# Hybrid decoder step on one core: order of the Winograd products, of the weights' sums and loads, of a tile ring, and of the opening

## Chip, cores, metric

The kernel runs on one core of one Trainium2 chip, as one launch. The metric is the device time in microseconds, as the median of several executions. TensorE is called PE here, its weight loads PEld, VectorE DVE, ScalarE ACT, GpSimd POOL and SyncE SP, as in the profile.

## The reference

One inference step of a decoder layer in fp32: 16 meta rows and a prompt of 512 rows, and 8 sample rows, model width 2048.

```
hp = layer_norm([meta; x_prompt]);  hs = layer_norm(x_sample)
z  = h @ w_in + b_in        -> q (16 x 64) | k (4 x 64) | v (4 x 64) | pool input u (1024)
a  = sliding-window attention with sinks;  p = multi-scale causal pooling of u
h1 = layer_norm(ALPHA * h + [a, p] @ w_o)
ff = (silu(h1 @ w_gate) * (h1 @ w_up)) @ w_down      # 2048 -> 5632 -> 2048
y  = layer_norm(ALPHA * h1 + ff)
```

It returns y of the prompt and of the samples, the last 128 rotated keys and values, and the last 15 pooling inputs.

## The kernel before

**Precision.** Each fp32 product is made of three passes in a faster fp32 format: an operand is split into a high and a low part, and `products` (L200 to L206) issues weight-high x data-high (L203), weight-high x data-low (L204), weight-low x data-high (L206). `split` (L183) makes the parts of 512 weight columns: the high part is a ScalarE copy (L187), the low part a VectorE subtraction (L188). They go into a ring of five slots each (`WB`), taken in the order of the code.

**Stages.** Opening (normalise x, transpose it, k and v projections, 0 to some 60 us); q and u projections with attention and pooling; output projection and first normalisation (to some 530 us); the gate and up projections (to 1457 us); the down projection (to 1875 us); last normalisation.

**Opening.** The loop over h (two halves of the columns) and g (four groups of rows of w_in), n = 4h + g + 1, places per round: `x_split` of an odd pair of row blocks (VectorE L372, ScalarE L375 and L378, VectorE L379), `x_norm` (ScalarE L341), `kv_mm`, the transposes `x_turn`, splits of three weight blocks, `x_split` of an even pair, `kv_mm`, the split of the fourth block. Each `step` keeps its instructions on PE, VectorE and ScalarE behind those of the step before. `later` holds the statistics of the row blocks 2 and 3 (VectorE L310, two at each `next`), which `normalisers(1)` and `x_norm(1, 0)` need.

**Gate and up.** 44 column blocks are taken as 22 pairs; each pair has a gate set g and an up set u. A `Set` multiplies a 2 x 2 block of weights (four tiles of 128 x 1024 floats, `q(r, c)`, loaded by L180 into `raw`, a ring of six slots) with 2 x 2 blocks of h1 in the Winograd form of Strassen: seven products P1 to P7, each of 8 x 3 = 24 matmuls of 128 x 260. The data operands are ready (`bop`: b11, b21, b22, t1 to t4, which P1, P2, P3, P5, P6, P7, P4 use). The weights need four sums on VectorE (`weight_sum`, L196), made in place of a loaded tile: S3 = A11 - A21 for P7, one from it for P6, one for P5, one for P3. Banks of PSUM: `al` holds P1, then P6, P5, P3 in turn; `ga` holds P7, then P4; `de` holds P2. VectorE or ScalarE reads a bank after a product, and a product that adds to it or starts it anew must come behind that read: L1024 reads P7 (`c22 = ga + p1`), L1030 P6, L1038 P2, L1043 P5, L1047 P4, L1052 P3.

Three kinds of sets: g0 and u0 are *kept* (P1 and P2 were made ahead and stand in PSUM); the up sets u1 and those of the next nine pairs are *filled* (P1 was made ahead and stands in SBUF, so six products are left); all others make seven. The order in the code of `run` before: kept P7 P6 P5 P4 P3, filled P2 P7 P6 P4 P5 P3, others P1 P7 P6 P2 P5 P4 P3.

**What sets the order on an engine.** A list scheduler of the framework orders each engine's instructions when the kernel is built, by readiness in its own timing and by priority; loads, splits and sums are raised by 400 instructions (`WPRIO`). `weight_sum` also stays behind the last low part that was split before it in the code. So an engine's order can differ from that of the code: PE in fact takes P2 of a gate set before its P6 where the input of P6 is late. The queue of loads on SP is one line, in the scheduler's order.

**Rows.** `row_tile` takes rows of 520 floats from a ring of 16 slots for x, later for z1 and, with 14 slots (`bufs`), for the gate and up stage: eight rows a pair (two of `go`, p of g, two of `uo`, p of u, `t12` and `t34`), six in the pairs of PLAIN, the last two. Slots are handed out in turn from `rows[2]`.

**Down.** `load_w(c, j)` (L1197, L1203) loads the weights of one column pair and, for c = 0, the two h1 tiles of accumulator j, which take the place of rows (accumulator j stands where slots 2j and 2j + 1 stood). `load_ops` (L1186) loads the operands into the 56 slots of `bop`. These all stand in one order on SP: `load_w(0, 0)`, ten operands, `load_w(0, 1)`, 25 operands, `load_w(0, 2)`, `load_w(0, 3)`. `column_pair` makes seven products of 15 matmuls; two column pairs start interleaved.

Of the kernel before, what the change touches and what calls it, by code (L numbers as in the profile page):

```python
# [31 lines left out]
NPAIR = F_TILES // 2  # L32
# [35 lines left out]
def hybrid_step(ctx, tc, xin, w_in, w_o, w_g, w_u, w_d, w_pool, par_d, cst_d, ident_d, ln2gb, kct_d, vc_d, hist_d,  # L68
                ck_d, cv_d, sp_d, yp, ys, nkp, nvp, npp, nks, nvs, nps):
    nc = tc.nc  # L70
# [184 lines left out]
    with ExitStack() as sa:  # L255
# [185 lines left out]
        for h in range(2):  # L441
            for g in range(4):
                n = h * 4 + g + 1
                with step(*three):
                    x_split(h, 2 * g + 1)
                    if n < 8 and n != 4:
                        x_norm(n // 4, n % 4)
                with step(*three):
                    kv_mm(h, 2 * g)
                if n < 8:  # L450
                    with step(*three):
                        x_turn(n // 4, n % 4)
                        if n < 7:
                            load_kvw((n + 1) % 4)
                        kvw.pop(n % 4, None)
                        kv_weights(n % 4, range(3))
                if h == 0 and g < 2:
                    with step(*three):
                        next(later.pop(0))
                if n < 8:  # L460
                    with step(*three):
                        x_split(n // 4, 2 * (n % 4))
                if n == 2:
                    with step(*three):
                        for x in later:
                            next(x)
                if n == 3:
                    with step(*three):
                        norm[1] = normalisers(1)
                        x_norm(1, 0)  # L470
                with step(*three):
                    kv_mm(h, 2 * g + 1)
                    if n < 8:
                        kv_weights(n % 4, [3])
            with step(*three):
                for i in range(4):
                    if i % 2:
                        nc.vector.tensor_scalar(zkv[i][:, XH[h]], out[i], par[:, PBIAS + i:PBIAS + i + 1], None,
                                                op0=ALU.add)
                    else:  # L480
                        nc.scalar.activation(zkv[i][:, XH[h]], out[i], AF.Identity, bias=par[:, PBIAS + i:PBIAS + i + 1])
                if h == 0:
                    out = kv_banks(1)
# [467 lines left out]
    class Set:  # L951


        def __init__(self, w, i, name):
            self.w, self.i, self.name = w, i, name
            self.raw, self.bk, self.p1 = {}, {}, None

        def q(self, r, c):
            if (r, c) not in self.raw:
# [4 lines left out]
        def s(self, t, a, b, op):  # L964
            weight_sum(op, self.q(*t), self.q(*a), self.q(*b))
            return self.q(*t)

        def prod(self, n, bk, first=True):


            b = {1: "b11", 2: "b21", 3: "b22", 4: "t4", 5: "t1", 6: "t2", 7: "t3"}[n]
            src = {1: lambda: self.q(0, 0), 2: lambda: self.q(0, 1), 4: lambda: self.q(1, 1),
                   7: lambda: self.s((1, 0), (0, 0), (1, 0), nc.vector.tensor_sub),
                   6: lambda: self.s((1, 0), (1, 1), (1, 0), nc.vector.tensor_sub),
                   5: lambda: self.s((0, 0), (1, 0), (0, 0), nc.vector.tensor_add),
                   3: lambda: self.s((0, 1), (0, 1), (1, 0), nc.vector.tensor_sub)}[n]()
            for g in range(2):
                wh, wl = split(src[:, g * 512:(g + 1) * 512], f"{self.name}_{n}{g}")
                for kk in range(4):
                    k = 4 * g + kk  # L980
                    sl = slice(kk * P, (kk + 1) * P)
                    hi, lo = bop[b][k // 2]
                    products([bk], wh[:, sl], wl[:, sl], [hi[:, k % 2, :]], [lo[:, k % 2, :]], k == 0 and first, k == 7, True)
# [17 lines left out]
        def run(self, c11, c12, c21, c22, side=(), out=None):  # L1001
# [12 lines left out]
                al = bank(f"p1_{self.name}")  # L1014
            ga = bank(f"p7_{self.name}")
            next(side, None)
            if filled and de is None:

                de = bank(f"p2_{self.name}")
                self.prod(2, de)  # L1020
            self.prod(7, ga)
            next(side, None)
            if filled:
                nc.vector.tensor_add(c22, ga, self.p1)  # L1024
            else:
# [2 lines left out]
            next(side, None)  # L1028
            if filled:
                nc.vector.tensor_add(c21, al, self.p1)  # L1030
                self.prod(4, ga, False)
            else:
                nc.scalar.copy(c21, al)
                if de is None:
                    de = bank(f"p2_{self.name}")
                    self.prod(2, de)
            next(side, None)
            nc.vector.tensor_add(c11, de, self.p1)  # L1038
            if out:
# [1 line left out]
            self.prod(5, al, False)  # L1041
            next(side, None)
            nc.vector.tensor_add(c22, c22, al)  # L1043
            if not filled:
                self.prod(4, ga, False)
            next(side, None)
            nc.vector.tensor_add(c21, c21, ga)  # L1047
# [68 lines left out]
        bop[n] = [(slot(f"{n}h{i}"), slot(f"{n}l{i}")) for i in range(4)]  # L1116
    turn = [i for i in range(NPAIR) if i not in PLAIN] + [*PLAIN]
    sets = [Set(w, i, f"{n}{i}") for i in turn for n, w in (("g", w_g), ("u", w_u))]
    g1 = ln1(1, zs1)
    fills = [s.ahead(n) for n in (1, 2) for s in sets[:NKEEP]]  # L1120
    for j, s in enumerate(sets[NKEEP + 1::2][:NFILL]):
# [20 lines left out]
    nxt = raws[2] % NRAW  # L1142
    raws[0] = raws[0][nxt:] + raws[0][:nxt] + [(fr, end[0])]
    raws[2] = 0
    rows[0] = [x for x in order if x[1] not in end]
    rows[2] = 0
    bufs.update(raw=NRAW + 1, row=14)
    side = ()
    for j, i in enumerate(turn):
# [362 lines left out]
```

## Time and profile before

| | us |
|---|---|
| three runs, median (lowest to highest) | 1950.8 (1949.04 to 1953.36) |
| the profiled execution | 1951.08 |
| its span, first to last instruction | 1949.3 |
| PE busy | 1897.8 |
| DVE busy | 1545.2 |
| ACT busy | 936.7 |
| mean granted clock of TensorE, share of full | 0.993 |

Times in the trace are counted from the start of the span. Matmuls are pipelined and their ends are modelled: a matmul of 128 x 260 is shown as 0.28 us long, while one starts every 0.12 us, so an idle time printed in front of a matmul is some 0.16 us shorter than what was lost from start to start. In a timeline a line is start, length, engine, line of the code, operation, out<-in, count, and in brackets the idle time of the engine before it with what ended it. In a list of stretches the five busy times are of PE, PEld, DVE, ACT and POOL.

### The profile page before, as it was taken

The numbers are of one execution on the slowest core, as the hardware profiler recorded it, in microseconds if no ns is written. First come the engines' busy times: TensorE is split into PE (matmuls) and PEld (weight loads), VectorE is DVE, ScalarE is ACT, GpSimd is POOL, SyncE is SP. The second block draws the span as 40 slices with busy tenths as digits, with TensorE's granted clock in tenths as the row PEclk, the third lists the DMA queues.
The fourth block names the chain that finished last, engine by engine and source line by source line (L and its number), as shares of the span: only waits on it lengthen the run. The fifth ranks groups of instructions, "written<-read, shape, count | busy, mean of one in ns | idle before, by whom it ended". The sixth has DMA issues, their size and how long they took to land.

```text
span 1949.3 us, 39269 instructions
## 1 busy us (share of the span) xinstructions
PE 1897.8 (97%) x15533; PEld 1867.3 (96%) x15533; DVE 1545.2 (79%) x2734; ACT 936.7 (48%) x1808; POOL 2.7 (0%) x9
## 2 busy tenths in 40 slices
PE   8999999999999999999999999999998999999996
PEld 8999999999989999999999999999998999999996
DVE  6765657768678888888888888888867888888878
ACT  6644445545555444444455555555544433443441
POOL 0000000000000000000000000000000000000000
PEclk9999999999999999999999999999999999999998
DMA  8722222766754545454545445453539564655232
GB/s 268 240 96 73 65 80 72 223 200 198 226 173 163 163 142 165 134 180 135 170 137 181 135 148 162 145 172 126 184 129 399 200 219 167 224 174 202 93 98 88
DMA packets 145240, 319.27 MB, mean 164 GB/s; under 512 B 14288, under 2 KB 66232, under 8 KB 144952
## 3 DMA queue, kind: packets, MB, share of 16 engines
q1 hardware_dynamic: 144480, 315.71, 48.9%
q8 instruction: 122, 2.00, 0.4%
q10 hardware_dynamic: 576, 1.05, 0.2%
q14 instruction: 62, 0.51, 0.1%
HBM read 265.22 MB, written 54.03 MB: 164 GB/s over the span
## 4 chain that ended last, share of the span: by engine, by line
PE 88%; DVE 5%; DMA 2%; ACT 2%; issue 1%; ACTq 0%; SPq 0%; DVEq 0%
PE p_g L203 7%; PE p_g L204 7%; PE p_g L206 7%; PE tri L206 6%; PE tri L203 6%; PE p_u L203 6%; PE tri L204 6%; PE p_u L204 6%; PE p_u L206 6%; PE o L203 3%; PE o L206 3%; PE o L204 3%; PE p_u L990 2%; DVE rr L188 2%; PE mm_u L203 2%; PE mm_u L206 2%
## 5 line engine op out<-in xcount | busy, mean ns | idle before, releaser
L187 ACT CAST rr<-fr 128x512 fp32r<-128x512 f32 (+1 forms) x1056 | 654.4, 643 | 807.5 <-DVE fr L196 269.2
L188 DVE TENSOR_TENSOR rr<-fr,rr 128x512 fp32r<-128x512 f32 (+1 forms) x1056 | 734.4, 716 | 252.2 <-ACT rr L187 238.8
L196 DVE TENSOR_TENSOR fr<-fr 128x1024 f32<-128x1024 f32 (+1 forms) x304 | 319.4, 1051 | 27.7 <-DMA fr<-in_w_u_dram 21.6
L203 PE MATMUL p_g<-rr 128*128 128x260 f32 x830 | 235.3, 285 | 7.9 <-ACT rr L187 6.4
L206 PE MATMUL p_g<-rr 128*128 128x260 f32 x830 | 230.6, 282 | 0.0
L203 PE MATMUL p_u<-rr 128*128 128x260 f32 x770 | 218.2, 284 | 6.5 <-DVE fr L1024 6.3
L204 PE MATMUL p_g<-rr 128*128 128x260 f32 x788 | 221.7, 282 | 0.0
L206 PE MATMUL p_u<-rr 128*128 128x260 f32 x770 | 215.2, 282 | 0.0
L204 PE MATMUL p_u<-rr 128*128 128x260 f32 x748 | 210.8, 283 | 0.0
L203 PE MATMUL tri<-rr 128*128 128x260 f32 x696 | 198.1, 285 | 4.9 <-ACT rr L187 3.9
L206 PE MATMUL tri<-rr 128*128 128x260 f32 x696 | 197.6, 284 | 1.9 <-DVE rr L188 1.9
L204 PE MATMUL tri<-rr 128*128 128x260 f32 x696 | 197.4, 284 | 0.0
L203 PEld LDWEIGHTS p_g<-rr 128*128 128x128 f32 x830 | 156.2, 188 | 10.2 <-ACT rr L187 8.5
L206 PEld LDWEIGHTS p_g<-rr 128*128 128x128 f32 x830 | 155.1, 189 | 0.0
L203 PEld LDWEIGHTS p_u<-rr 128*128 128x128 f32 x770 | 144.9, 188 | 8.1 <-issue 8.1
L204 PEld LDWEIGHTS p_g<-rr 128*128 128x128 f32 x788 | 148.1, 188 | 0.0
L203 PE MATMUL o<-rr 128*128 128x260 f32 x512 | 145.0, 284 | 0.3 <-ACT rr L187 0.3
L206 PEld LDWEIGHTS p_u<-rr 128*128 128x128 f32 x770 | 144.7, 189 | 0.0
L204 PE MATMUL o<-rr 128*128 128x260 f32 x512 | 144.0, 282 | 0.0
L206 PE MATMUL o<-rr 128*128 128x260 f32 x512 | 143.6, 282 | 0.2 <-DVE rr L188 0.2
L204 PEld LDWEIGHTS p_u<-rr 128*128 128x128 f32 x748 | 140.7, 188 | 0.0
L203 PEld LDWEIGHTS tri<-rr 128*128 128x128 f32 x696 | 131.8, 189 | 5.4 <-ACT rr L187 5.4
(320 smaller groups left out, 4564.4 us busy)
## 6 DMA issues: line engine op xcount, KB each, us to landing
fr<-in_w_u_dram SPq DMA_DIRECT2D x100, 512.0 KB
fr<-in_w_g_dram SPq DMA_DIRECT2D x90, 512.0 KB
fr<-in_w_d_dram SPq DMA_DIRECT2D x64, 640.0 KB
t_d<-fr SPq DMA_DIRECT2D x140, 260.0 KB
fr<-in_w_o_dram SPq DMA_DIRECT2D x64, 512.0 KB
fr<-in_w_in_dram SPq DMA_DIRECT2D x48, 512.0 KB
rr<-t_d SPq DMA_DIRECT2D x87, 260.0 KB
mid_b<-t_d SPq DMA_DIRECT2D x53, 260.0 KB
```

The lines of the kernel that those rows point to most:

```text
L187: nc.scalar.copy(wh, s)
L188: last_lo[0] = (lo or nc.vector).tensor_sub(wl, s, wh.bitcast(F32)).ins
L196: i = op(*args).ins
L203: nc.tensor.matmul(o, wh, hi[j], start=first, stop=False, skip_group_check=onto)
L204: nc.tensor.matmul(o, wh, lo[j], start=False, stop=False, skip_group_check=onto)
L206: nc.tensor.matmul(o, wl, hi[j], start=False, stop=last, skip_group_check=onto)
L990: nc.tensor.matmul(bk, self.q(0, n - 1)[:, k * P:(k + 1) * P], z1[0][4 * (n - 1) + k // 2][:, k % 2, :], start=(k == 0), stop=(k == 7))
```

## The change

In the gate and up stage a set may make S3 early (`early`): an unfilled set while P1's weights are split, between the two halves; a filled or kept set while P3 of the set before it is split. Filled sets begin with P7 and then P2; kept sets take P4 ahead of P5. With S3 early, a filled set loads its tiles in the order A21, A11, A12, A22 instead of A12, A21, A11, A22. The ring of rows is put in the order of addresses and starts at slot 10 (-172 modulo 14), so that the last row handed out is the last slot. In the opening the statistics of row blocks 2 and 3 and the second normalisation move behind the second `kv_mm` and the last split of their round, one, two and one `next` in the first three rounds.

```diff
--- before.py
+++ after.py
@@ -454,24 +454,20 @@
                             load_kvw((n + 1) % 4)
                         kvw.pop(n % 4, None)
                         kv_weights(n % 4, range(3))
-                if h == 0 and g < 2:
-                    with step(*three):
-                        next(later.pop(0))
                 if n < 8:
                     with step(*three):
                         x_split(n // 4, 2 * (n % 4))
-                if n == 2:
-                    with step(*three):
-                        for x in later:
-                            next(x)
-                if n == 3:
-                    with step(*three):
-                        norm[1] = normalisers(1)
-                        x_norm(1, 0)
                 with step(*three):
                     kv_mm(h, 2 * g + 1)
                     if n < 8:
                         kv_weights(n % 4, [3])
+                if n < 4:
+                    with step(*three):
+                        for _ in range((1, 2, 1)[g]):
+                            next(later.pop(0))
+                        if n == 3:
+                            norm[1] = normalisers(1)
+                            x_norm(1, 0)
             with step(*three):
                 for i in range(4):
                     if i % 2:
@@ -953,7 +949,7 @@
 
         def __init__(self, w, i, name):
             self.w, self.i, self.name = w, i, name
-            self.raw, self.bk, self.p1 = {}, {}, None
+            self.raw, self.bk, self.p1, self.s3, self.next = {}, {}, None, False, None
 
         def q(self, r, c):
             if (r, c) not in self.raw:
@@ -965,17 +961,27 @@
             weight_sum(op, self.q(*t), self.q(*a), self.q(*b))
             return self.q(*t)
 
+        def early(self):
+
+            self.s((1, 0), (0, 0), (1, 0), nc.vector.tensor_sub)
+            self.s3 = True
+
         def prod(self, n, bk, first=True):
 
 
             b = {1: "b11", 2: "b21", 3: "b22", 4: "t4", 5: "t1", 6: "t2", 7: "t3"}[n]
             src = {1: lambda: self.q(0, 0), 2: lambda: self.q(0, 1), 4: lambda: self.q(1, 1),
-                   7: lambda: self.s((1, 0), (0, 0), (1, 0), nc.vector.tensor_sub),
+                   7: lambda: self.q(1, 0) if self.s3 else self.s((1, 0), (0, 0), (1, 0), nc.vector.tensor_sub),
                    6: lambda: self.s((1, 0), (1, 1), (1, 0), nc.vector.tensor_sub),
                    5: lambda: self.s((0, 0), (1, 0), (0, 0), nc.vector.tensor_add),
                    3: lambda: self.s((0, 1), (0, 1), (1, 0), nc.vector.tensor_sub)}[n]()
             for g in range(2):
                 wh, wl = split(src[:, g * 512:(g + 1) * 512], f"{self.name}_{n}{g}")
+                if g == 0 and n == 1:
+                    self.early()
+                if g == 0 and n == 3 and self.next and (self.next.p1 is not None or self.next.bk):
+
+                    self.next.early()
                 for kk in range(4):
                     k = 4 * g + kk
                     sl = slice(kk * P, (kk + 1) * P)
@@ -1014,12 +1020,12 @@
                 al = bank(f"p1_{self.name}")
             ga = bank(f"p7_{self.name}")
             next(side, None)
-            if filled and de is None:
-
+            self.prod(7, ga)
+            next(side, None)
+            kept = de is not None
+            if filled and not kept:
                 de = bank(f"p2_{self.name}")
                 self.prod(2, de)
-            self.prod(7, ga)
-            next(side, None)
             if filled:
                 nc.vector.tensor_add(c22, ga, self.p1)
             else:
@@ -1028,12 +1034,13 @@
             next(side, None)
             if filled:
                 nc.vector.tensor_add(c21, al, self.p1)
+            else:
+                nc.scalar.copy(c21, al)
+            if filled or kept:
                 self.prod(4, ga, False)
             else:
-                nc.scalar.copy(c21, al)
-                if de is None:
-                    de = bank(f"p2_{self.name}")
-                    self.prod(2, de)
+                de = bank(f"p2_{self.name}")
+                self.prod(2, de)
             next(side, None)
             nc.vector.tensor_add(c11, de, self.p1)
             if out:
@@ -1041,7 +1048,7 @@
             self.prod(5, al, False)
             next(side, None)
             nc.vector.tensor_add(c22, c22, al)
-            if not filled:
+            if not (filled or kept):
                 self.prod(4, ga, False)
             next(side, None)
             nc.vector.tensor_add(c21, c21, ga)
@@ -1116,6 +1123,8 @@
         bop[n] = [(slot(f"{n}h{i}"), slot(f"{n}l{i}")) for i in range(4)]
     turn = [i for i in range(NPAIR) if i not in PLAIN] + [*PLAIN]
     sets = [Set(w, i, f"{n}{i}") for i in turn for n, w in (("g", w_g), ("u", w_u))]
+    for a, b in zip(sets, sets[1:]):
+        a.next = b
     g1 = ln1(1, zs1)
     fills = [s.ahead(n) for n in (1, 2) for s in sets[:NKEEP]]
     for j, s in enumerate(sets[NKEEP + 1::2][:NFILL]):
@@ -1142,8 +1151,9 @@
     nxt = raws[2] % NRAW
     raws[0] = raws[0][nxt:] + raws[0][:nxt] + [(fr, end[0])]
     raws[2] = 0
-    rows[0] = [x for x in order if x[1] not in end]
-    rows[2] = 0
+
+    rows[0] = sorted((x for x in order if x[1] not in end), key=lambda x: x[1])
+    rows[2] = -(6 * NPAIR + 2 * (NPAIR - len(PLAIN))) % 14
     bufs.update(raw=NRAW + 1, row=14)
     side = ()
     for j, i in enumerate(turn):
```

## Rows read from the trace of the kernel before

**Rows 1.** The page: busy shares (part 1), VectorE's low parts (part 5)

```profile
PE 1897.8 (97%) x15533; PEld 1867.3 (96%) x15533; DVE 1545.2 (79%) x2734; ACT 936.7 (48%) x1808; POOL 2.7 (0%) x9
...
L188 DVE TENSOR_TENSOR rr<-fr,rr 128x512 fp32r<-128x512 f32 (+1 forms) x1056 | 734.4, 716 | 252.2 <-ACT rr L187 238.8
```

**Rows 2.** Stretches: us, busy us (instructions) of each engine, granted clock, DMA share, GB/s

```profile
1025.12:1428.12 403.00, 403.00 (x3360) 403.00 (x3361) 341.41 (x525) 213.40 (x408) 0.00 (x0) 1.00 0.47 155
...
590.70:1025.12 434.42, 420.00 (x3458) 416.12 (x3456) 375.24 (x594) 212.72 (x403) 0.00 (x0) 1.00 0.48 154
...
1457.07:1514.86 57.79, 49.69 (x376) 48.26 (x377) 40.47 (x57) 25.50 (x39) 0.00 (x0) 0.94 0.99 383
...
1514.86:1778.07 263.21, 263.21 (x2198) 263.21 (x2197) 223.37 (x314) 107.48 (x151) 0.00 (x0) 1.00 0.59 205
...
749.27:1025.12 275.85, 265.74 (x2184) 263.04 (x2184) 238.16 (x379) 132.86 (x253) 0.00 (x0) 1.00 0.48 155
...
618.60:641.58 22.98, 22.98 (x194) 22.98 (x193) 20.48 (x34) 12.70 (x24) 0.00 (x0) 1.00 0.59 196
```

**Rows 3.** Waits of PE, whole span: us in total, times, longest us

```profile
PE p_g L203 <- ACT rr L187: 6.4, 10, 0.6
...
PE p_u L203 <- DVE fr L1024: 6.3, 7, 1.1
```

**Rows 4.** Timeline of one filled up set: PE, VectorE (start, us; idle before)

```profile
755.43 0.28 PE L203 MATMUL p_g<-rr 128*128 128x260 f32 x1
...
757.63 1.23 DVE L196 TENSOR_TENSOR fr<-fr 128x1024 f32<-128x1024 f32 x1 [2.46 <-DMA fr<-in_w_u_dram]
...
765.98 1.22 DVE L196 TENSOR_TENSOR fr<-fr 128x1024 f32<-128x1024 f32 x1
...
767.12 0.42 DVE L1024 TENSOR_TENSOR fr<-p_u,fr 128x260 f32<-128x260 f32 x1
...
767.69 0.36 PE L203 MATMUL p_u<-rr 128*128 128x260 f32 x1 [0.80 <-DVE fr L1024]
```

**Rows 5.** Timeline of the SP queue around one filled pair

```profile
730.21 0.33 SPq L180 DMA_DIRECT2D fr<-in_w_u_dram  x1
...
751.33 0.51 SPq L180 DMA_DIRECT2D fr<-in_w_u_dram  x1
...
770.76 2.38 SPq L180 DMA_DIRECT2D fr<-in_w_g_dram  x2
```

**Rows 6.** Timeline of one gate set: ScalarE and PE at P4

```profile
748.60 0.62 ACT L187 CAST rr<-fr 128x512 fp32r<-128x512 f32 x1 [0.81 <-PE p_g L204]
...
749.27 0.39 PE L203 MATMUL p_g<-rr 128*128 128x260 f32 x1 [0.64 <-ACT rr L187]
```

**Rows 7.** Timeline of g0: VectorE and PE before P3

```profile
602.42 1.22 DVE L196 TENSOR_TENSOR fr<-fr 128x1024 f32<-128x1024 f32 x1
...
603.55 0.42 DVE L1043 TENSOR_TENSOR fr<-fr,p_g 128x260 f32<-128x260 f32 x1
...
604.12 0.36 PE L203 MATMUL p_g<-rr 128*128 128x260 f32 x1 [1.49 <-DVE fr L1043]
```

**Rows 8.** Timeline of the SP queue, last set and after

```profile
1429.75 20.84 SPq L1203 DMA_DIRECT2D fr<-h_d  x2
...
1450.69 2.28 SPq L1186 DMA_DIRECT2D rr<-t_d  x5
...
1456.53 1.03 SPq L1197 DMA_DIRECT2D fr<-in_w_d_dram  x2
```

**Rows 9.** Timeline of PE, start of the down projection

```profile
1463.60 0.59 PE L203 MATMUL tri<-rr 128*128 128x260 f32 x1 [3.18 <-ACT rr L187]
...
1497.03 0.39 PE L203 MATMUL tri<-mid_b,rr 128*128 128x260 f32 x1 [1.80 <-DVE fr L1230]
```

**Rows 10.** Timeline of VectorE and PE in the opening

```profile
25.83 1.28 DVE L310 BATCH_NORM_STATS2 mid_a<-fr 128x6 f32<-128x512 f32 x2
...
28.36 0.53 PE L203 MATMUL kv<-rr 128*128 128x276 f32 x2 [0.96 <-ACT rr L378]
```

## Prediction

> **What bounds the kernel now.** The page comes first: PE is busy for 97% of the span [rows 1], so a change can win only what PE loses in places. The question is where PE loses time, and the stretches answer it [rows 2]. With two unfilled sets a pair, from 1025.12 to 1428.12 us, PE runs 3360 matmuls in 403.00 us, 0.1199 us each, with no idle time: that is the pace when nothing is missing, and 24 matmuls (one product) are 2.88 us. The earlier stretch, 590.70 to 1025.12, where the up sets of ten pairs are filled, holds 3458 matmuls in 434.42 us. At 0.1199 they are 414.8, so **19.7 us are lost**. The third stretch is the start of the down projection: 376 matmuls in 57.79 us, where the steady down projection has 2198 in 263.21 (0.1198 each, 45.0 for 376). There **12.8 us are lost**, at a granted clock of 0.94.
>
> Who ends the waits [rows 3]: first matmuls of gate products wait ten times for a ScalarE high part (L187), of up products seven times for VectorE's L1024. The reader is to see that these are two causes with one period: seven pairs take 275.85 us, 39.4 each, against 312 x 0.1199 = 37.4 [rows 2], so 2.0 us a pair.
>
> **The change part by part.** The number of products, sums, splits and loads is unchanged, so all of it is order.
>
> *Up sets begin with P7.* In a filled up set P4 restarts the bank of P7, which L1024 must have read. The order on PE is P2, P7, P6, P4, so L1024 has one product (2.88 us). At 767.69 PE waits for it: VectorE was idle up to 757.63 for a load, then had splits and sums in a row, the last one at 765.98, ahead of L1024 at 767.12 [rows 4]. After the change the order is P7, P2, P6, P4: L1024 has two products, 5.76 us, and needed 2.88 plus 0.80. So this wait goes. Its sum: the 19.7, less the gate waits and the one of g0 below, is 8.5 us. What is late next is L1030, which must read P6's bank before P5 adds to it, with one product (P4) between, as before. I take 7.5 us, bounds 3 (L1030 inherits part of it) and 8.5.
>
> *S3 one product ahead.* Before, S3 of an up set waits 2.46 us for a load [rows 4]. The raw ring has six slots and a set takes four: the first two loads go into slots that have been free for a whole set, the third and fourth into those of the set just ending. The queue shows it: for this set (0,1) was issued at 730.21, while (0,0), its third, left at 751.33 [rows 5]. The new order of loads is (1,0), (0,0), (0,1), (1,1), so S3's two inputs come 20 us early and the late one belongs to P2, one product later. S3 itself (1.22 us of VectorE) only moves: in front of the second low part of P3 (or of P1, in unfilled sets), where splits run ahead of PE.
>
> *The gate waits.* At 749.27 PE needs the first high part of P4, and ScalarE makes it only at 748.60, when a product has let go of its slot [rows 6]. That slot, five splits back, was P6's second half. P6 ran last because its input (1,1) came late: it goes into the slot of the up set's first load, (0,1), which is free only after the last split of that set, and the two loads of this kind leave at 770.76 and after 772.8 [rows 5]. After the change the first load is (1,0), which the sum of P3 lets go, some 2 us earlier. The one gate set in the stretch whose predecessor already loads in the new order is g1, behind the kept u0: 194 matmuls in 22.98 us, no idle time [rows 2]. Start to start the wait is 0.92, and the next two matmuls are late by 0.15 together: 0.95 us, ten times, 9.5. I take 7.5; bounds 0 (order on PE and slots unchanged) and 9.5.
>
> *Kept sets.* In g0 the sum for u0's P7 (602.42) stands ahead of L1043 (603.55), on which P3 waits until 604.12: 1.49 us idle, 1.65 over the pace [rows 7]. S3 made a product ahead stands before the end of P5 and no longer there; L1043 still lies open between P5 and P3, 0.42 and the way there. I take 1.0, bounds 0 and 1.65.
>
> *Row ring.* The SP queue is one line. At 1429.75 it issues half of the first accumulator's h1, then stands 20 us for a row that the last up set still uses; the ten operand loads start at 1450.69, the weights of the second column pair at 1456.53 [rows 8]. PE waits for these weights until 1463.60 [rows 9] and the clock falls. Turned, the last pair has rows 8 to 13, and rows 0 to 7, which the accumulators 0 to 3 take, are free a pair (40 us) earlier. The next thing the queue waits for is the operands' own slots: b11 after P1 of the last set, about 1439.8 (1457.07 [rows 2] less 6 products of 2.88 us), t3 after P7, 1442.7, and so on. So the loads start 11 us earlier, over a DMA system that is nearly idle, and keep ahead: five operands of 260 KB in 3.6 us of two interleaved products are 370 GB/s, and the stretch moved 383 [rows 2]. What stays: the first split of the new pool waits for the last matmul of the old one (about 1.2 us), and the bursts of two pairs starting together on VectorE (the wait on L1230 at 1497.03, 1.80 us [rows 9], is of that kind). I take 9.0 of the 12.8 us; bounds 5 and 11.
>
> The Trainium skill ("DMA: Bandwidth & Descriptors", Specifications) puts what a core gets from HBM at about 358 GB/s. By that the 22.1 MB of this stretch (57.79 us at 383 GB/s) would take 61.8 us, 4 us more, which the head start would still cover; the trace shows more than the page allows, and the row decides.
>
> *Opening.* The statistics of the later rows move behind x_split and the last split of a step. At 25.83 they hold up x_split by 1.28 us, and PE waits 0.96 at 28.36 [rows 10]; that goes. But the same work then stands, undiminished, before the next x_split, and the normalisers and x_norm now come behind the last split instead of ahead of it. VectorE's chain through this stretch keeps its length but for that, so most is given back by 52 us. I take 0.5; bounds -0.5 and 2.
>
> *Sum.* 7.5 + 7.5 + 1.0 + 9.0 + 0.5 = 25.5 us. The profiled execution took 1951.1 us (span 1949.3), 0.3 over the median of 1950.8, so 1925.3 on the median.
>
> **Rivals.** *The gate waits stay*, since slots and not loads set them: P4's first part still finds P6's slot taken. For it: a pattern alike to the hundredth ten times over. Against: g1. 1925.3 + 7.5 = 1932.8.
>
> *L1030 takes L1024's place*: it has the slack L1024 had, and VectorE does 238.16 us in seven pairs, 34.0 of what would then be 37.4, 91% against 85% (341.41 of 403.00) where nothing is lost [rows 2]. Against: its backlog came from the 2.46 us wait. 1932.8 as well.
>
> *The start of the down projection is bound by VectorE*, not by loads, and gives back 4: 1930.
>
> *The schedule in the pair stays as it is*: the order on each engine is made by a list scheduler with weight work raised in priority, and may come out with the old waits. Then only the row ring and opening pay: 1950.8 - 9.5 = 1941.3.
>
> *Slower: S3 blocks VectorE.* It is queued ahead of P3's second low part. If it waited for a load as it does now (until 757.63 [rows 4]), that part would be ready at 757.63 + 1.22 + 0.72 (a split's low part [rows 1]) = 759.6, where PE, in P3 from 755.43 [rows 4], needs it after 14 matmuls, at 757.1: 2.5 us in each of ten pairs, 25 us. With the gate waits kept, 1950.8 - 9.0 - 0.5 - 7.5 + 25 = 1958.8. It decides from the point where the second load lands after 757.1 - 0.72 - 1.22 = 755.2. The issue times of [rows 5] speak against it by some 20 us. The Trainium skill ("PSUM — Partial Sum Buffer", Engine vs sequencer instructions) calls VectorE's queue a strict FIFO, the rule by which this would happen; the trace agrees, since L1024 sat behind a sum it does not need.
>
> **How the numbers follow.** Forecast 1925 at 0.46; gates stay 0.17; L1030 0.13; VectorE at the down start 0.10; schedule unchanged 0.08; slower 0.06. All low bounds together save 3 + 0 + 0 - 0.5 + 5 = 7.5 (1943), all high ones 8.5 + 9.5 + 1.65 + 11 + 2 = 32.7 (1918). The range 1917 to 1941 leaves out the slower case and part of the unchanged one. Measurement tells 0.2%, 3.9 us, from no change; every case but the slower one is past it, with a little kept for partial mixtures: faster 0.91, same 0.03, slower 0.06.
>
> **What would show it.** Right: a filled pair of 37.5 to 38 us instead of 39.4, no wait on L1024, no p_g wait of 0.64 before P4; operand loads from about 1440 and no PE idle over 1.5 us at 1457 to 1500, clock 1.00. Wrong: up sets waiting at P7 on an L187 or L196; a wait on L1030 of like size; VectorE idle for a load between P3's two low parts; operand loads still issued after 1450.

## The result, and the profile after

The changed kernel takes **1932.4 us** (median of 4 runs, 1931.94 to 1932.89) against 1950.6 for the kernel before in the same runs: a ratio of 0.9905, 95% interval 0.9888 to 0.9922. That is 18.2 us less. The forecast was 1925, 25.5 us less. The profiled execution took 1932.89 us, its span 1931.1.

Divided at the starts of the same matmuls (g0's first; the 3459th from there, which lies in the gate set behind the last filled pair, just behind that set's wait before P4; the first and the 377th of the down projection, and so on), the profiled executions stand like this, in us:

| stretch | before | after | difference |
|---|---|---|---|
| first transpose to the end of the opening | 80.15 | 80.39 | +0.24 |
| from there to g0 | 494.48 | 494.50 | +0.02 |
| filled pairs, with the kept pair ahead of them (3458 matmuls) | 434.77 | 426.37 | -8.40 |
| unfilled pairs | 432.27 | 432.28 | +0.01 |
| start of the down projection (376 matmuls) | 57.23 | 47.21 | -10.02 |
| the next 2198 matmuls | 263.56 | 263.56 | 0 |
| last stretch | 155.90 | 156.16 | +0.26 |

So two stretches paid, and they are the two that the forecast named. First the page of the changed kernel (part 1, PE's line) and the stretches (us, busy us and instructions of each engine, then granted clock, DMA share and GB/s):

```profile
PE 1894.4 (98%) x15533; PEld 1865.8 (97%) x15533; DVE 1539.9 (80%) x2734; ACT 944.1 (49%) x1808; POOL 2.7 (0%) x9
```

```profile
15.89:96.28 80.39, 76.94 (x585) 74.33 (x585) 58.36 (x111) 52.86 (x99) 0.00 (x0) 0.94 0.77 249
...
590.78:1017.15 426.37, 418.83 (x3460) 416.00 (x3459) 370.36 (x593) 214.41 (x402) 0.00 (x0) 1.00 0.50 157
1017.15:1449.43 432.28, 431.54 (x3601) 431.33 (x3599) 362.81 (x558) 232.68 (x437) 0.00 (x0) 1.00 0.49 163
1449.43:1496.64 47.21, 45.90 (x376) 45.31 (x377) 37.09 (x53) 23.26 (x35) 0.00 (x0) 1.00 0.96 355
```

The down projection starts at full clock now (1.00, 0.94 in [rows 2]). In the filled pairs 3458 matmuls at 0.1199 us would be 414.6, so 11.8 us are still lost there. The waits of PE in that stretch (us in total, times, longest) say to what:

```profile
PE p_g L203 <- ACT rr L187: 7.1, 11, 0.6
PE p_g L203 <- ACT fr L1038: 0.3, 1, 0.3
PE p_u L203 <- ACT rr L187: 0.2, 1, 0.2
```

The waits on L1024 and L1043 of [rows 3, 7] are gone. (The change moves lines: what was L1024, the addition of P7's bank and the kept P1, is L1030 after.) The gate waits of [rows 3] are not: they were ten and are **eleven**, at the same 0.64 us. The new one is g1's, the very set on whose lack of a wait the forecast leaned.

L1030 (old L1024) in one filled up set, VectorE's timeline: its bank is read at 684.05, and P4 restarts the bank at 688.55 without a wait.

```profile
684.05 0.42 DVE L1030 TENSOR_TENSOR fr<-p_u,fr 128x260 f32<-128x260 f32 x1
...
688.55 0.28 PE L203 MATMUL p_u<-rr 128*128 128x260 f32 x1
```

The SP queue at the start of the down projection, which [rows 8] show of before (start us, us for issuing, line): the ten operands leave at 1429.31, 20.1 us ahead of the first matmul (1449.43); before, 7.1 us ahead (1450.69 against 1457.74).

```profile
1429.31 2.49 SPq L1196 DMA_DIRECT2D rr<-t_d  x5
1431.90 2.78 SPq L1196 DMA_DIRECT2D mid_b<-t_d  x5
1435.51 0.33 SPq L1207 DMA_DIRECT2D fr<-in_w_d_dram  x1
```

### The profile page after: what moved, and what is told of

The parts are those of the page before. It is cut to its first block, busy times and chain, and to the rows that moved or that the text cites. A ratio compares the mean times of both kernels' runs of the same rounds, so it can differ in the third digit from the quotient of the medians.

```text
span 1931.1 us, 39334 instructions
## 1 busy us (share of the span) xinstructions
PE 1894.4 (98%) x15533; PEld 1865.8 (97%) x15533; DVE 1539.9 (80%) x2734; ACT 944.1 (49%) x1808; POOL 2.7 (0%) x9
## 4 chain that ended last, share of the span: by engine, by line
PE 92%; DVE 4%; ACT 2%; DMA 1%; issue 1%; SPq 0%; DVEq 0%; ACTq 0%
PE p_g L203 7%; PE p_g L204 7%; PE p_g L206 7%; PE p_u L203 7%; PE p_u L206 7%; PE p_u L204 7%; PE tri L203 7%; PE tri L206 7%; PE tri L204 7%; PE o L203 3%; PE o L206 3%; PE o L204 3%; PE p_u L996 2%; PE mm_u L203 2%; PE mm_u L206 2%; PE mm_u L204 2%
```

## Experiments on the two stretches that paid

Every stretch named below is divided like those of the table, and comes from one profiled execution of its kernel. Stretches that an edit does not touch differ between executions all the same: the 494 us ahead of g0 took 493.0 to 496.1, the last stretch 155.9 to 157.7. Single edits are therefore read from their own stretch, and the measured ratio stands beside it.

**The row ring alone.** The kernel before, with

```
-    rows[0] = [x for x in order if x[1] not in end]
-    rows[2] = 0
+    rows[0] = sorted((x for x in order if x[1] not in end), key=lambda x: x[1])
+    rows[2] = -(6 * NPAIR + 2 * (NPAIR - len(PLAIN))) % 14
```

> The kernel before with the row ring turned and nothing else. Theory (the parts pay in separate stretches and add up): the first 376 matmuls of the down projection took 57.2 us before and 47.2 us after the whole change, so this alone gives 10.0 us: 1940.5 us, operand loads issued from about 1440 us, granted clock 1.00 there, every wait of the up projection as before. Rival (part of the 10 us came from VectorE reaching the down projection with less backlog, through the earlier S3): 1943 to 1947 us, with waits of 0.7 us or more left at the start of the down projection beyond those of the changed kernel.

Measured: ratio 0.9952 (0.9939 to 0.9965), 1943.1 us against 1951.7. The start of the down projection took 47.18 us (after: 47.21), at clock 1.00; the operands left at 1437.80, 20.1 us ahead of the first matmul at 1457.93, and the filled pairs kept their waits on L1024 and on the gates.

```profile
1437.80 2.23 SPq L1186 DMA_DIRECT2D rr<-t_d  x5
```

```profile
1457.93:1505.11 47.18, 45.88 (x376) 45.29 (x377) 36.93 (x52) 23.20 (x35) 0.00 (x0) 1.00 0.95 349
```

The 10.0 us are the ring's alone; nothing of them came from the earlier S3. With the old ring this stretch took 55.25 to 57.48 us in five kernels, so it varies by some 2 us with what else is changed; with the ring turned it took 47.18 to 47.22 in six. The time is 8.5 us under the kernel before rather than 10.0; in the profiled execution the difference lies in stretches that the edit does not touch (ahead of g0 496.0 us instead of 494.5, the tail 157.3 instead of 155.9, the filled pairs 433.6 instead of 434.8).

**The ring turned half way.** As above, but six slots short (`- 6` inside the bracket), so that the last pair uses rows 2 to 7: the first accumulator's rows are free, the second's are not.

> The kernel before with the row ring turned so that the last pair uses rows 2 to 7 instead of 12, 13 and 0 to 3. Theory (the SP queue stands at the first accumulator whose row is still in use): the first accumulator, the first ten operands and the weights of the second column pair are issued from about 1440 us, the queue then stands at the second accumulator until about 1450, and the other operands follow: the first 376 matmuls of the down projection take 47 to 51 us instead of 57.2. Rival (only a ring that is free for all four accumulators helps): 55 to 57 us.

Measured (one execution): the start of the down projection took 52.27 us, half of the gain, a little beyond the range of the theory and short of the rival's. The queue shows why:

```profile
1437.86 2.23 SPq L1186 DMA_DIRECT2D rr<-t_d  x5
...
1442.65 1.27 SPq L1197 DMA_DIRECT2D fr<-in_w_d_dram  x2
1455.60 2.45 SPq L1080 DMA_DIRECT2D a_d<-fr  x2
1458.15 1.95 SPq L1203 DMA_DIRECT2D fr<-h_d  x2
1460.19 2.77 SPq L1186 DMA_DIRECT2D mid_b<-t_d  x6
```

The first ten operands and the weights of the second column pair go out early, then the line stands from 1443.9 to 1455.6 and the other operands follow at 1460.19, where they left at 1445.80 with the ring fully turned. What the line stands at is not yet a load: it is the two stores of the last pair's own results (L1080). They read rows 2 and 3, the ones that the second accumulator takes, so here they come ahead of its loads (1458.15); with the ring fully turned the stores leave only behind the second accumulator's loads, at 1470.18 and 1473.22. The queue stands at the first transfer that can't start yet, and the operands behind it, whose slots are free, wait too.

**P7 first, without the early S3.** The kernel before with the new order of products in `run`, that of the kept sets too, and nothing else (the removed lines are left out here):

```
+            self.prod(7, ga)
+            next(side, None)
+            kept = de is not None
+            if filled and not kept:
                 de = bank(f"p2_{self.name}")
                 self.prod(2, de)
...
+            if filled or kept:
                 self.prod(4, ga, False)
```

> The kernel before with P7 ahead of P2 in filled up sets and the order 7,6,4,5,3 in kept sets; S3 is not made early. Theory (it is the second product ahead of L1024's deadline that pays): the waits on L1024 go, 8.5 us, the waits of the gate sets stay, g0 keeps 0 to 1.65 us of its wait: 1942.1 us (1940.5 to 1943). Rival (the earlier S3 is what clears VectorE's queue): S3 of the up set is then still made just ahead of P7, P7 is first in the set, and PE waits for its split: 1945 to 1952 us.

Measured: ratio 0.9972 (0.9960 to 0.9983), 1946.6 us; the filled pairs took 429.99 us, 4.8 less than before. The waits on L1024 are gone, eleven gate waits stand, and something new stands before P5 in five of the sets. PE's and VectorE's timelines of one of them (the page's releaser is in brackets):

```profile
691.70 0.42 DVE L1030 TENSOR_TENSOR fr<-p_u,fr 128x260 f32<-128x260 f32 x1
...
692.27 0.36 PE L203 MATMUL p_u<-rr 128*128 128x260 f32 x1 [0.80 <-ACT rr L187]
```

The split that the row names as releaser is that of P3 (it began at 691.55). What P5 needed is L1030 (here the addition that reads P6's bank), done at 692.12, 0.15 us before PE goes on. This is the prediction's rival "L1030 takes L1024's place", and it is real when S3 is made inside the set. The time falls into the range of the rival expected here, but not for its reason: no up set waits at P7. Between P7 and P5 VectorE has the same three sums as in the changed kernel, only later: L1030 ends 6.6 us after P6's first matmul (692.12 against 685.56), in the changed kernel the same addition (L1036) 5.0 us after it (690.70 against 685.66), and P5 is due 5.8 us after it. The sum for P6 already comes 1.5 us later (3.2 us ahead of P6's first matmul instead of 4.8); what delays it was not tried.

**The early S3, without P7 first.** The kernel before with `early()` and its calls, P2 still first:

> The kernel before with S3 made one product ahead, P2 still first in filled up sets. Theory (the order P7, P2, P6, P4 pays, not the earlier S3): L1024 still has one product; its waits shrink but do not go, since the backlog of the 2.46 us wait for a load is gone: half of 8.5 us, and the 1.65 us of g0 go: 1944.7 us. Rival (backlog was the whole cause): all 8.5 and 1.65 us go: 1940.4 us. Second rival (backlog had no part): 1949 us.

Measured: **slower**, ratio 1.0020 (1.0010 to 1.0030), 1956.2 us; the filled pairs took 439.95 us, 5.2 more than before. None of the three expectations was right. ScalarE's timeline of one up set, and what stood before P4 there:

```profile
680.13 1.66 ACT L187 CAST rr<-fr 128x512 fp32r<-128x512 f32 x3 [5.34 <-DMA fr<-in_w_u_dram]
```

```profile
690.13 0.42 DVE L1034 TENSOR_TENSOR fr<-p_u,fr 128x260 f32<-128x260 f32 x1
...
690.69 0.36 PE L203 MATMUL p_u<-rr 128*128 128x260 f32 x1 [0.49 <-ACT rr L187]
```

Making S3 early puts (1,0) and (0,0) into the two raw slots that are free a set ahead. (0,1) becomes the third load, and P2, still the first product, is now the one that waits for it: ScalarE stands idle for 5.34 us, P2's first split starts at 680.13, just ahead of P2 at 680.97, and its low part is late by 0.15 to 0.22 us in each set. P4 still waits for the addition after P7 (L1034 here, done at 690.55), 0.66 us over the pace in each of nine sets.

The two edits with each other, as the time of the filled pairs:

| | S3 where it was | S3 one product ahead |
|---|---|---|
| P2 first | 434.8 | 440.0 |
| P7 first | 430.0 | 426.4 |

Alone they give -4.8 and +5.2, together -8.4. (The last cell is the changed kernel, which has the ring and the opening too; with the ring alone this stretch differs by 1.2 from the kernel before, by 0.2 and 0.4 with the ring half turned and with the opening alone, so steps of that size mean nothing.) They are one edit: the early S3 has its two inputs loaded first, and then P7, which needs nothing else, has to be the first product.

**The early S3 with the old order of loads**, that is with (0,1) asked for ahead of S3's inputs in filled sets:

```
         def early(self):
+            if self.p1 is not None:
+                self.q(0, 1)
             self.s((1, 0), (0, 0), (1, 0), nc.vector.tensor_sub)
```

> The kernel before with S3 made one product ahead, P2 still first in filled up sets, and the load of (0,1) asked for ahead of (1,0) and (0,0), as before the change. Theory (S3 stands in VectorE's line ahead of P3's second low part, and its third load lands some 20 us later than its first two): the slower rival of the prediction happens here, 2.5 us in each of ten filled pairs or more, 1965 to 1980 us. Rival (the early S3 costs by its place alone, load or no load): 1956 us, like the early S3 with the new order of loads. Second rival (the load lands in time): 1945 us.

Measured (one execution): 1964.0 us, the filled pairs 447.90, 13.1 more than before. VectorE waits for loads 46 us in that stretch (before 21.6, after none):

```profile
DVE fr L196 <- DMA fr<-in_w_g_dram: 23.3, 10, 3.8
...
DVE fr L196 <- DMA fr<-in_w_u_dram: 22.9, 12, 3.8
```

```profile
761.86 1.23 DVE L196 TENSOR_TENSOR fr<-fr 128x1024 f32<-128x1024 f32 x1 [3.31 <-DMA fr<-in_w_u_dram]
763.00 0.69 DVE L188 TENSOR_TENSOR rr<-fr,rr 128x512 fp32r<-128x512 f32 x1
```

The row at 761.86 is S3; VectorE stands idle for 3.31 us until its load has landed. So the early S3 does wait when the loads come in the old order, and the time is close to the theory's 1965. But the slower rival of the prediction did not happen as it was calculated. In VectorE's line S3 stands here behind both low parts of P3 and ahead of a low part of P2 (763.00), and PE runs P3 (759.96 to 762.84) and the start of P2 without a wait. The cost is 1.3 us a pair instead of 2.5, and PE pays later: in this pair at P4, for the addition of P7's bank (1.14 us idle at 772.72, a wait that the kernel before has too), and in the next gate set at P7 (1.00 at 785.46) and P6 (0.48 at 791.38), where the kernel before has none. The Trainium skill ("PSUM — Partial Sum Buffer", Engine vs sequencer instructions) has VectorE's queue as a strict FIFO; the trace agrees, since the low part, whose split was made at 758.34, starts only as S3 ends (763.00 against 761.86 + 1.23).

## Experiments on the gate waits

Why does a gate set wait before P4? The changed kernel, set g2, ScalarE's, VectorE's and PE's timelines (start, us; idle before and its releaser):

```profile
660.54 0.62 ACT L187 CAST rr<-fr 128x512 fp32r<-128x512 f32 x1 [0.26 <-PE p_u L204]
...
670.44 0.62 ACT L187 CAST rr<-fr 128x512 fp32r<-128x512 f32 x1 [0.81 <-PE p_g L204]
```

```profile
661.20 0.69 DVE L188 TENSOR_TENSOR rr<-fr,rr 128x512 fp32r<-128x512 f32 x1 [0.38 <-ACT rr L187]
661.93 1.23 DVE L196 TENSOR_TENSOR fr<-fr 128x1024 f32<-128x1024 f32 x1
...
664.51 1.22 DVE L196 TENSOR_TENSOR fr<-fr 128x1024 f32<-128x1024 f32 x1
665.65 0.42 DVE L1097 TENSOR_TENSOR fr<-fr 128x260 f32<-128x260 f32 x1
665.99 0.68 DVE L188 TENSOR_TENSOR rr<-fr,rr 128x512 fp32r<-128x512 f32 x1
```

```profile
671.11 0.39 PE L203 MATMUL p_g<-rr 128*128 128x260 f32 x1 [0.64 <-ACT rr L187]
```

The sum for P6 (661.93) waits for no load. It follows the low part of P7's second half (661.20), whose input it overwrites; that half's high part (660.54) had to wait for a slot which P3 of the up set before still used. P6's own low part comes behind the sum for P5, at 665.99. Meanwhile PE has P2 in full, and P6 goes behind it: the order on PE is P7, P2, P6 but for a few matmuls. Then P6's second half is the last thing ahead of P4, whose first split (670.44) wants that slot. It was no different in the kernel before. VectorE's nine waits for loads in this stretch (21.6 us) were all for up weights, and in a gate set the sum for P6 followed P7's low part at once:

```profile
778.53 0.69 DVE L188 TENSOR_TENSOR rr<-fr,rr 128x512 fp32r<-128x512 f32 x1
779.26 1.22 DVE L196 TENSOR_TENSOR fr<-fr 128x1024 f32<-128x1024 f32 x1
```

In the next four kernels `behind_pe`, an argument added to `prod`, puts the first matmul of the named weight block (product, block) behind the named matmul in PE's order.

**P4 behind P5.** The changed kernel with P4's first two matmuls, which stand where the wait is, put behind P5 by an order on PE (no wait on a semaphore; the comments here are not in the code):

```
-                self.prod(4, ga, False)
+                self.prod(4, ga, False, behind_pe={(4, 0): m5})    # m5: P5's last matmul
```

> The changed kernel, with the first two matmuls of P4 behind P5 in sets that begin with P1, where the gate waits stand. Theory (with P6 last on PE, P5 can't start either: it adds to P6's bank, which ScalarE's L1038 reads only once P6 has ended; the two matmuls of P4 only fill that time): PE waits for L1038 instead, P5 starts when it does now or 0.3 us earlier, and P4's two matmuls come on top: 1932 to 1935 us. Rival (only P4's slot is late): the eleven waits go, 1922 us.

Measured: ratio 0.9909 (0.9893 to 0.9924), 1933.8 us; the filled pairs took 428.31 us, 1.9 more than the changed kernel. PE's waits in the stretch are now eleven on L1043 (L1038 in the changed kernel: ScalarE's copy of P6's bank):

```profile
PE p_g L203 <- ACT fr L1043: 10.6, 11, 1.4
```

That is what the theory said. Both products that could follow P6 hang on P6's end, P4 by its slot and P5 by its bank. Swapping them only changes the name of the wait.

**Half of P2 behind P6.** The changed kernel, P2's matmuls from the fifth of its eight weight blocks on (12 of 24) behind P6's last, again as an order on PE alone:

```
-                self.prod(2, de)
+                self.prod(2, de, behind_pe={(2, 4): m6})           # m6: P6's last matmul
```

> The changed kernel, with one thing more: in sets that begin with P1, the second half of P2 (its last 12 matmuls) is put behind P6 on PE; nothing else moves. Theory (the gate waits come from P6 being the last product on PE before P4, whose first half takes the split slot of P6's second half): the slot is free 1.4 us earlier, the eleven waits of about 0.95 us go, the stretch from g0 to the last filled set's gate takes 416 us instead of 426.4, and the time is 10.4 us under the changed kernel: ratio 0.985 to the kernel before, about 1922 us. Rival (the step of the prediction: the waits follow from the late load of (1,1), so that P6 itself is late): the wait moves to P6 or stays, 1932 us.

Measured: ratio 0.9887 (0.9870 to 0.9903), 1929.2 us; the filled pairs took 421.73 us, 4.6 less than the changed kernel. No gate wait is left, as the theory had it, but only half of its gain came. P6's third matmul now waits for its low part, eleven times:

```profile
PE p_g L206 <- DVE rr L188: 3.9, 11, 0.7
```

**All of P2 behind P6**: `(2, 0)` in place of `(2, 4)`.

> The changed kernel, with the whole of P2 behind P6 in sets that begin with P1. Theory as for the half: the gate waits go, and as the sum for P6 is queued behind P7's last low part, P6 starts on time or waits up to 0.3 us in each of eleven sets: 1922 to 1925 us. Rival (P6's input is late by its load): PE waits at P6 by 1 us or more a set, 1932 us or more.

Measured (one execution): 1958.1 us, the filled pairs 451.49, 25.1 more than the changed kernel: the theory was wrong in this point and the rival right in its size, though not in its cause. VectorE's timeline, PE's wait, and two pairs of this kernel (an early and a later one):

```profile
828.35 1.22 DVE L196 TENSOR_TENSOR fr<-fr 128x1024 f32<-128x1024 f32 x1
829.49 0.42 DVE L1102 TENSOR_TENSOR fr<-fr 128x260 f32<-128x260 f32 x1
829.82 0.68 DVE L188 TENSOR_TENSOR rr<-fr,rr 128x512 fp32r<-128x512 f32 x1
...
830.56 0.39 PE L206 MATMUL p_g<-rr 128*128 128x260 f32 x1 [1.77 <-DVE rr L188]
```

```profile
628.60:668.05 39.45, 37.67 (x313) 37.47 (x313) 33.37 (x53) 19.07 (x35) 0.00 (x0) 1.00 0.49 155
789.57:830.56 40.99, 39.21 (x312) 39.01 (x312) 34.30 (x55) 19.61 (x36) 0.00 (x0) 0.96 0.48 149
```

P6's low part (829.82) stands in VectorE's line behind the sum for P5 (828.35) and a side addition, not behind a load. An idle stretch of this kind stands ahead of both pairs shown, 2.11 us ahead of the early one and 1.77 ahead of the later. Behind the first two of the eleven the granted clock stayed at 1.00; behind each of the others it fell to 0.50 for a few us, 0.96 over the pair, and that costs 1.5 us a pair more.

**Nine matmuls of P2 behind P6**: `(2, 5)`.

> The changed kernel, with the last 9 matmuls of P2 behind P6 in sets that begin with P1 (12 in the run before this kind). With 12 the gate waits went, but P6's third matmul waited 0.48 us over the pace for its low part. Theory (two ends pull on P2: what stands ahead of P6 covers its low part, what stands behind it covers P4's slot, which wants about 0.95 us): three matmuls (0.36 us) more ahead of P6, 9 (1.08 us) behind it: 0.1 to 0.2 us are left of each wait, a filled pair takes 37.5 to 37.7 us, the up stretch 417 to 418.5 us instead of 421.7, the time 1925.5 us, ratio 0.987 to 0.986. Rival (P6's low part moves with P2, as VectorE's order follows PE's): the wait on the low part stays at 0.48 us, 1929 us.

Measured: ratio **0.9863** (0.9847 to 0.9880), 1924.4 us, the best of all kernels here. The filled pairs took 418.12 us:

```profile
589.29:1007.41 418.12, 417.71 (x3460) 415.63 (x3459) 370.12 (x591) 215.95 (x401) 0.00 (x0) 1.00 0.49 160
```

That is 3.5 us over 3458 x 0.1199 = 414.6, and clearly less than the 421.73 with 12 matmuls behind P6. From P6 of one gate set to P6 of the next (701.65 to 739.30 us) a filled pair takes 37.65 us, where the pace gives 37.4; the changed kernel took 38.36 (from P4 at 671.11 to P4 at 709.47), the kernel before 39.4 [rows 2]. Only g1 still shows a wait for P6's low part (0.3 us). Two direct tests of the cause were not made: a sixth split slot, and VectorE making P6's low part ahead of the sum for P5.

## The opening

The kernel before with the other order of the opening and nothing else (the loop of the diff).

> The kernel before with the other order of the opening and nothing else. In the changed kernel PE's idle time up to 57 us is 4.8 us instead of 6.6, yet g0 starts at 590.78 instead of 590.70, because the granted clock was 0.50 at 20 to 24 us and 0.61 at 52 to 56 us. Theory (the order brings its 1.8 us and the clock takes them back by chance of the start, not by the order): without a fall of the clock 1948.8 us, with one 1950.6 us. Rival (the chain through VectorE keeps its length, as the prediction had it): 1950.6 us, g0 at 590.7 whether the clock falls or not. Both within 0.2% of the kernel before.

Measured: ratio 0.9992 (0.9983 to 1.0001), 1950.1 us: no difference that can be told. The opening took 79.30 us in its profiled execution, 0.85 less than before. Neither theory nor rival named that; but the other profiled executions agree on it. With the old order the opening took 80.10 to 80.15 us in six kernels, with the new one 79.06 to 79.30 in five (the kernels with P2 or P4 moved among them). The sixth is the changed kernel itself, with 80.39, and there the granted clock stood at half for a while:

```profile
20.00:24.00 4.00, 4.00 (x19) 4.00 (x19) 3.55 (x7) 4.00 (x8) 0.00 (x0) 0.50 1.04 378
52.00:56.00 4.00, 4.00 (x22) 4.00 (x22) 3.25 (x6) 2.91 (x7) 0.00 (x0) 0.61 0.48 140
```

So the new opening is worth 1.0 us, and this one execution gave it back: from the first transpose to the 201st matmul it took 29.95 us, the kernel with the opening alone, whose clock did not fall there, 28.90 with the same order of instructions. The fall at 20 to 24 us is not the order's: the kernel with only the row ring, which has the old opening, shows 0.61 there (and lost nothing by the 101st matmul, 16.12 us as in the kernel before). A fall at 52 to 56 us shows in three of six executions with the new order and in none of six with the old one, and in two of the three the opening took 79.14 and 79.30 us. Whether the order invites it stays open.

## Why the prediction was right, and where it was not

The time lay inside the range, but not at the forecast: it is the value of the rival *the gate waits stay* (1932.8, chance 0.17), and that rival's reason, slots and not loads, is what the experiments bear out. The forecast's own sum failed in one of its three large terms. By the steps of the prediction:

- **L1024 with two products' time**: right, and a little low in size. Forecast 7.5, all 8.5 us went. L1030 did not inherit anything in the changed kernel. It does when S3 stays inside the set (429.99 us of the P7-first kernel), so the rival was held off by the early S3, which the prediction put down as a mere move. It took both edits to be rid of the one wait without the other, and the prediction did not say so.
- **Loads and S3**: right. S3 waits for no load, and the order of loads is why: with the old one VectorE waits 46 us (early S3, (0,1) first). The prediction did not see that the early S3 without P7 first would cost 5.2 us, because it took the two as separate parts. Its slower rival did not come in its own form in any run.
- **The gate waits**: wrong, forecast 7.5, measured -0.9 (eleven waits for ten). The step that failed is "P6 ran last because its input (1,1) came late". The sum for P6 shows no wait for a load, in the changed kernel and in the kernel before (the description of the kernel, where it calls P6's input late, is wrong in the same way). P6 is late since P7's second half waits for a slot and VectorE makes its low part behind other sums. The evidence was g1, taken as the set "whose predecessor already loads in the new order". But g1 differed in a second way: u0's P3 ran in the midst of its P1, ahead of all of P7, and only two matmuls of P2 came ahead of P6. In the kernel with P7 first alone, u0 and g1 load as before, but u0's P3 comes behind g1's P1, P2 goes ahead of P6 but for a few matmuls, and g1 waits like the others (0.64 us at 632.73). One set that differs in two ways can't tell which of them matters. A filled pair therefore takes 38.36 us, not the 37.5 to 38 that were to show the forecast right. What the waits do answer to is shown by moving P2: 12 matmuls of it behind P6 take the gate waits away, 24 bring a worse one, 9 leave nearly none. Why the scheduler puts P2 first was argued from the rows above, not tried by itself.
- **Kept sets**: forecast 1.0. The 1.65 us of g0 went; g1's new wait, in two places 0.80 and 0.46 us over the pace, is the eleventh counted above, and eats most of it.
- **Row ring**: right. Forecast 9.0, measured 10.0 (alone 10.05). The operands left 20.1 us ahead of the first matmul (1457.74 in the kernel before, where the prediction's stretch begins at 1457.07) instead of 7.1, more than the 17 that the slots' dates gave. The DMA system that was called nearly idle was busy for 0.29 and moved 94 GB/s from 1428.12 to 1457.07 us; there was room all the same, and the waits of 1.80 us that I kept as VectorE's shrank too: 0.79 is left of them.
- **Opening**: forecast 0.5; 1.0 in five executions, -0.24 in the one that was profiled for the changed kernel. Less is given back than the prediction thought: the kernel with nine matmuls of P2 moved, which has this opening at full clock, is 2.3 us ahead of the kernel before at the 176th matmul from the first transpose, and still 1.0 at the end.

Summed by stretch: 8.4 + 10.0 - 0.5 (opening, tail and the rest of the table) = 17.9 us; the other 0.3 of the span's 18.2 lie ahead of the first transpose and behind the last matmul. What is missing against 25.5 is in the main the gate waits' 7.5, and with them put right by moving nine matmuls of P2 the kernel takes 1924.4.

## What to carry to other kernels

When the order of loads, of sums and of products each have one line, change them as one: the first two loads go into the slots that are free first, so they must belong to the product that runs first; of the two halves of this change one alone lost 5.2 us and the other gave 4.8 of the 8.4. The wait that repeated here to the hundredth of a microsecond was one of order, not of transfer. Where you see one, look at what PE does just ahead of it and who holds the slot, and split a product around the culprit so that one part covers what is late before it and the other covers the slot behind it. A load in a single queue that has to wait for its slot blocks all that follow it, so give the first loads of the next stage the slots that the last users of the old stage don't hold.

## What the runs showed of the hardware

- With all of P2 behind P6, PE stood idle once in 39 to 41 us. Behind the first two of these stretches (2.11 and 1.77 us) TensorE's granted clock stayed at 1.00. Behind each of the next nine (1.77 us) it fell to the lower of its two levels (1.2 against 2.4 GHz; matmuls 0.22 us apart instead of 0.12) for a few us, 0.96 over a pair. Idle stretches of 0.64 us (the changed kernel) and 0.92 us (P4 behind P5), once in 38 to 39 us, left it at 1.00. What tells the first two from the nine is not shown.
- In the opening the clock fell to between 0.50 and 0.81 over 4 us in four of twelve profiled executions and not in the others, among them kernels with the same order of instructions on PE, VectorE and ScalarE up to there.
- The releaser in brackets was wrong twice where PE waits for two semaphores: a split that belongs to another product was named, while the addition in VectorE's line ended 0.14 to 0.15 us before PE went on.
- With the operands of the down projection issued early, the DMA system moved 355 GB/s over 47 us, 349 in the kernel with only the ring turned. The Trainium skill ("DMA: Bandwidth & Descriptors", Specifications) puts a core's share of HBM at about 358 GB/s. The same stretch moved 383 before the change [rows 2], so that figure is no ceiling here, and the measurement decides.
